# An attention head loop whose rows on ScalarE, VectorE, GpSimdE and the transfer queue are written out, instead of TensorE's alone

## The chip, the cores and the metric

One core of a Trainium2 chip runs the whole program. The metric is the device time of one execution in microseconds, as a median over runs. TensorE (PE) multiplies matrices, ScalarE (ACT) and VectorE (DVE) work on rows of 128 partitions, GpSimdE (POOL) does a few copies and products, and SyncE (SP) issues the transfers.

## The reference

Two residual layers on a sequence of 512 frames of width 1024, all in float32, each made of a token mixer and a gated feed-forward part behind a root-mean-square norm. The first layer mixes by causal means over four windows; the second by attention with 16 heads of width 64, with normed q and k, a learned bias by relative position, and a band of nine chunks of 64 frames:

```python
q = head_rmsnorm(q.reshape(B, S, N_HEADS, HEAD_DIM), q_norm)
k = head_rmsnorm(k.reshape(B, S, N_HEADS, HEAD_DIM), k_norm)
...
s = jnp.einsum('bqhd,bkhd->bhqk', qc, kb).astype(jnp.float32) * scale + bias[None]
s = jnp.where(valid[None, None, None, :], s, -1e30)
p = jax.nn.softmax(s, axis=-1).astype(vb.dtype)
return jnp.einsum('bhqk,bkhd->bqhd', p, vb)
...
return o @ w_o
```

The feed-forward part is `(silu(causal_dwconv3(h W_gate)) * (h W_val)) W_out` with 2816 inner channels. The order of the program is: pool mixer, feed-forward 0, attention, feed-forward 1. The change lies in `attention()` alone.

## The kernel before, in words

Every float32 product is made of three matmuls: each operand is split into a high part `hi` (rounded, by ACT) and a low part `lo` (the rest, by DVE), and `mm3` (L123 to L125) adds hi·hi, hi·lo and lo·hi. So most matmuls need a copy on ACT and then a subtraction on DVE before them.

*The head loop.* Its 64 tiles are (head h, query tile t of 128 frames); step i of the loop is called slot i, with i = 4h + t. In slot i the program issues `scores` of tile i (two matmuls `sc`, L1062 and L1063), `turn` of tile i - 2 (`tp`, transposes of the softmaxed tile, L1078), and, when i - 4 is the last tile of a head, `mix` of this head (`oo`, eight matmuls against the values, L1090). After the scores DVE adds the bias and takes the row's extreme (L1066), ACT takes the exponential with its row sum (L1068), DVE the reciprocal (L1069), ACT scales (L1070). After the transposes ACT copies the high part (`pt..h`, L102) and DVE takes the low part (`pt..l`, L103). After the mix ACT copies one half (`ob`, L1095) and DVE adds it (`o2`, L1096).

*Pairs.* Two heads make a pair. In slots 8m + 2 and 8m + 3 (`CM = (2, 3)`) the next pair's q and k are put channel-major by `channel_major`: four transposes (`zt`, L1032), the high part on ACT (`zh`, L107 for q, L1036 for k), then on DVE the low part of q (`zl`, L108) or the two low parts of k (`kl`, two instructions, L1039), a copy on POOL (L1043) and two transfers (L1046).

*PSUM.* All of `sc`, `tp`, `zt` and `oo` share a ring of four banks (tag S), in the order of their allocation. A tile that comes four allocations later waits until the last reader of the earlier one is done.

*Side work on TensorE.* Between these steps `fill` deals out matmuls of four long generators, by a due count: the q and k projections of pairs 2 to 7 (`project(1)` to `project(3)`, until slots 3.5, 19.5 and 35.5), then the output projection of pairs 0 to 5 (`outputs`, from slot 35.5 to 72): eight outputs `wo` of four pairs, then eight of two pairs. Pairs 6 and 7 come after the loop. A projection leaves four tiles z, copied on ACT (L966) or DVE (L964), squared on ACT (L956), reduced on DVE (L957), and normed by small operations and a product on POOL (L979). An output is added to the residual X on DVE (L1016). Each pair's mixed heads are split into `two..` (L102, L103) before the output projection reads them; two.. 0 and 1 hold the high parts of pairs 0 to 3, two.. 4 and 5 their low parts.

*What sets the order.* Only TensorE runs in the written order in this loop (`tc.manual_schedule(engines={PE})`). The rows of ACT, DVE, POOL and SP are set by a scheduler that places each instruction by readiness and priority as it sees them.

The due counts and the rings are these lines:

```python
FE = (3.5, 19.5, 35.5)
FO = LAG + 6
CM = (2, 3)
```

Of the kernel before, what the change touches and what calls it, by code (L numbers as in the profile page):

```python
# [17 lines left out]
F32 = mybir.dt.float32  # L18
# [54 lines left out]
def trunk(ctx: ExitStack, tc: tile.TileContext, xt, xT, cols, band, edge, poolw, gv, wout, wqk, wv, wo, rel, out):  # L73
# [15 lines left out]
    def psum(tag, name, bufs=2):  # L89
        return ps.tile([P, S], F32, name=name, tag=tag, bufs=bufs)  # L90
# [30 lines left out]
    def mm3(o, sh, sl, mh, ml, first, last, **how):  # L121

        yield nc.tensor.matmul(o, sh, mh, start=first, stop=False, **how)  # L123
        yield nc.tensor.matmul(o, sh, ml, start=False, stop=False, **how)  # L124
        yield nc.tensor.matmul(o, sl, mh, start=False, stop=last, **how)  # L125
# [791 lines left out]
    def attention():  # L917
# [75 lines left out]

            yield from products(ov, wv[half], f"wv{half}", evict=evict)

        def output(ps_, after=None):

            p0, p1 = ps_[0], ps_[-1] + 1
            n = (p1 - p0) * P
            nd = D // n  # L1000
            w = {}

            def load(d):
                eng = nc.gpsimd if p0 < 6 else None
                w[d] = load_split(wo[d:d + nd, :, p0 * P:p1 * P].rearrange("d p m -> p d m"), D, f"wo{d}_{p0}", eng=eng, eng_hi=eng)

            for d in range(KD):
                if d % nd == 0:
                    if d not in w:
                        load(d)  # L1010
                    hi, lo = w[d]
                o = psum("PQ"[d % 2], f"wo{d}_{p0}")
                for p in ps_:
                    s = slice(d % nd * n + (p - p0) * P, d % nd * n + (p - p0 + 1) * P)
                    yield from mm3(o, hi[:, s], lo[:, s], XS[p], XS[KD + p], p == p0, p == p1 - 1)
                nc.vector.tensor_add(X[d], o, X[d])  # L1016
                if after:
                    after(d)
                    if d == 1:
                        load(nd)  # L1020

        def outputs():
            yield from output(range(4))
            yield from output((4, 5))

        def channel_major(p, i):


            zt = psum("S", f"zt{p}_{i}", 4)
            for t in range(TT):  # L1030
                j = 4 * i + 2 * (p % 2)
                nc.tensor.transpose(zt[:, t * P:(t + 1) * P], Z[p // 2, t][:, j:j + 2, :].rearrange("p h d -> p (h d)"), ident)  # L1032
            zh, z2 = (big.tile([P, S], F32R, name=f"z{c}{p}_{i}", tag="zqk", bufs=8) for c in "h2")
            zl = None if i else g_tile(f"zl{p}_{i}")
            if i:
                nc.scalar.activation(zh, zt, AF.Copy, scale=gq[:, i:i + 1])  # L1036
                for e in range(2):
                    hs = slice(e * HD, (e + 1) * HD)
                    nc.vector.scalar_tensor_tensor(KL[p % 2][e][hs], zt[hs], gq[hs, i:i + 1], zh[hs].bitcast(F32), op0=OP.mult, op1=OP.subtract)  # L1039
            else:  # L1040
                split_scaled(zt, gq[:, i:i + 1], zh, zl)

            nc.gpsimd.tensor_copy(z2[HD:], zh[HD:].bitcast(F32))  # L1043
# [5 lines left out]
        def scores(h, t):  # L1049

            p, e = divmod(h, 2)
            q, k, kl = QK[p, 0][e], QK[p, 1][e], KL[p % 2][e]
            if t == 0:

                base = rdram[h, :]
                for r, n in ((0, S - HD), (HD, S)):
                    nc.sync.dma_start(BT[h % 2][r:r + HD, S - n:], bass.AP(tensor=base.tensor, offset=base.offset + HD, ap=[[1, HD], [1, n]]))
            n = (t + 1) * P
            nw = max(n, 256)

            sc = psum("S", f"sc{h}_{t}", 4)
            nc.tensor.matmul(sc[:, :nw], q[:, t * P:n], k[:, :nw], start=True, stop=False)  # L1062
            nc.tensor.matmul(sc[:, :nw], q[:, t * P:n], kl[:, :nw], start=False, stop=True)  # L1063
            SM[h, t] = s_ = big.tile([P, n], F32, name=f"sb{h}_{t}", tag=f"sb{t}")
            mx = tmp.tile([P, 3], F32, name=f"mx{h}_{t}", tag="mx", bufs=4)
            nc.vector.tensor_tensor_reduce(out=s_[:, :n], in0=sc[:, :n], in1=BT[h % 2][:, :n][:, ::-1], scale=1.0,  # L1066
                                           scalar=3e38, op0=OP.add, op1=OP.min, accum_out=mx[:, 0:1])
            nc.scalar.activation(s_[:, :n], s_[:, :n], AF.Exp, scale=-1.0, bias=mx[:, 0:1], accum_out=mx[:, 1:2])  # L1068
            nc.vector.reciprocal(mx[:, 2:3], mx[:, 1:2])  # L1069
            nc.scalar.activation(s_[:, :n], s_[:, :n], AF.Copy, scale=mx[:, 2:3])  # L1070

        def turn(h, t):

            n = (t + 1) * P
            s_ = SM.pop((h, t))
            tp = psum("S", f"tp{h}_{t}", 4)
            for j in range(t + 1):
                nc.tensor.transpose(tp[:, j * P:(j + 1) * P], s_[:, j * P:(j + 1) * P], ident)  # L1078
            split(tp[:, :n].rearrange("p (j q) -> p j q", q=P), *(x[:, t:4 * t + 1:3] for x in PT[h % 2]))

        def mix(h):

            p, e = divmod(h, 2)
            hs = slice(e * HD, (e + 1) * HD)
            oo = psum("S", f"oo{h}", 4)
            if p not in O2:
                O2[p] = big.tile([P, S], F32, name=f"o2_{p}", tag="o2", bufs=4)
            for c in range(2):
                for j in range(TT):
                    nc.tensor.matmul(oo[:, j * P:], V[j, h // 4][:, h % 4].rearrange("p a d -> p (a d)"),  # L1090
                                     PT[e][c][:, 4 * j:3 * j + TT].rearrange("p t q -> p (t q)"),
                                     start=j == 0 and c == 0, stop=j == TT - 1 and c == 1)
            ob = g_tile(f"ob{h}")
            other = slice(HD - e * HD, 2 * HD - e * HD)
            nc.scalar.activation(ob[hs], oo[other], AF.Copy)  # L1095
            nc.vector.tensor_add(O2[p][hs], oo[hs], ob[hs])  # L1096

        Z, QK, SM = {}, {}, {}
        rcol, r2, late = None, small("r2", TT), []
# [2 lines left out]
            late.pop(0)()  # L1102
        run(values(0, "PQ"))
        for i in range(2):
            channel_major(0, i)
        run(values(1, "SS"))


        tiles_ = [(h, t) for h in range(H) for t in range(TT)]
        nb = len(tiles_)  # L1110
        fillers = [(project(1), 96, -3, FE[0]), (project(2), 96, FE[0], FE[1]), (project(3), 96, FE[1], FE[2]), (outputs(), 144, FE[2], nb + FO)]

        with tc.manual_schedule(engines={mybir.EngineType.PE}):
            cur, done, kept = 0, 0, 0

            def fill(upto):

                nonlocal cur, done
                while cur < len(fillers):
                    g, n, a, b = fillers[cur]  # L1120
                    due = n * (upto - a) / (b - a)
                    while done < min(due, n):
                        next(g)
                        done += 1
                    if upto < b:
                        return
                    run(g)
                    cur, done = cur + 1, 0

            fill(0)  # L1130
            for i in range(nb + LAG + LAGM):
                steps = []
                if i < nb:
                    steps.append(lambda: scores(*tiles_[i]))
                if i % 8 in CM and i // 8 + 1 < NPAIR:
                    steps.append(lambda: channel_major(i // 8 + 1, CM.index(i % 8)))
                j = i - LAG
                if 0 <= j < nb:
                    steps.append(lambda: turn(*tiles_[j]))
                j2 = j - LAGM  # L1140
                if 0 <= j2 < nb and j2 % TT == TT - 1:
                    steps.append(lambda: mix(tiles_[j2][0]))
                for x, step in enumerate(steps):
                    step()
                    if late and x < 2:
                        late.pop(0)()
                    fill(i + (x + 1) / len(steps))

                while 8 * kept + 7 <= j2 and (cur == 3 or cur == 2 and done >= 24 * (kept // 2 + 1)):
                    split(O2[kept], XS[kept], XS[KD + kept])  # L1150
                    kept += 1
            fill(nb + FO)
        assert kept == NPAIR
        return lambda after: output((6, 7), after)

    def last_pairs(rest, c, name):

# [89 lines left out]
```

## Time and profile before

| | |
|---|---|
| median of 3 runs | 972.5 us (971.89, 972.5, 973.37) |
| the profiled execution | 972.12 us, of which its span is 970.3 us |
| PE busy | 961.6 us (99%) |
| DVE busy | 809.6 us |
| ACT busy | 576.6 us |
| POOL busy | 102.9 us |
| head loop, first scores to last mix | 452.5 to 606.3 us of the span |
| scores of slots 34, 42, 50 and 56 start | 538.85, 557.03, 573.11, 585.9 us |

Times in the traces are counted from the span's start. PE's busy share is high by construction: matmuls are pipelined and their ends are modelled, so a busy PE may still be waiting; the distance from one start to the next tells more. A group of a timeline (x2, x3) is several instructions of one form in a row.

### The profile page before, as it was taken

Reading aid. Unit: us, or ns where it says so; the run is one execution under the profiler, and the core shown is the slowest. Engines: PE = TensorE matmul, PEld = TensorE weight load, DVE = VectorE, ACT = ScalarE, POOL = GpSimd, SP = SyncE. Lnnn points to the kernel's source line nnn. Section 1 sums busy time; section 2 is a strip of 40 time slices with the busy share of each in tenths; the row PEclk is TensorE's granted clock in tenths of the full one; section 3 lists DMA queues with packets and bytes.
Section 4 is the critical chain, followed back from the end, with each engine's and each line's share of the span. In section 5 each row is a group of like instructions: output and inputs, shape, how many; then the busy total and the mean of one; then the engine's idle time right before and its main releaser. Section 6 shows DMA issues by size and latency. Waiting matters only on the chain.

```text
span 970.3 us, 13704 instructions
## 1 busy us (share of the span) xinstructions
PE 961.6 (99%) x4982; PEld 815.0 (84%) x4982; DVE 809.6 (83%) x1462; ACT 576.6 (59%) x990; POOL 102.9 (11%) x90
## 2 busy tenths in 40 slices
PE   8999999999999999999999999999999999999998
PEld 7788988888888888888888787888988888888886
DVE  8999999999899854442777888999999999989953
ACT  7665564655555544345898988646565565566531
POOL 2300000000000013204534532000000000000000
PEclk9999999999999999999999999999999999999999
DMA  9222332332323224232343341332233233332323
GB/s 342 77 93 71 114 113 75 120 120 92 105 76 120 78 84 147 94 121 91 111 115 107 97 118 55 101 108 80 94 114 104 87 120 108 104 103 77 116 79 109
DMA packets 37427, 102.82 MB, mean 106 GB/s; under 512 B 4432, under 2 KB 7904, under 8 KB 37360
## 3 DMA queue, kind: packets, MB, share of 16 engines
q1 hardware_dynamic: 37296, 101.90, 33.0%
q8 instruction: 39, 0.64, 0.3%
q14 instruction: 28, 0.23, 0.1%
q0 software_dynamic: 32, 0.04, 0.0%
q10 hardware_dynamic: 32, 0.00, 0.0%
HBM read 95.60 MB, written 2.14 MB: 101 GB/s over the span
## 4 chain that ended last, share of the span: by engine, by line
PE 94%; DVE 4%; ACT 2%; issue 0%; DMA 0%; DVEq 0%; ACTq 0%
PE st_m L610 11%; PE out L124 8%; PE out L123 8%; PE out L125 8%; PE st_m L612 6%; PE st_t L610 6%; PE gv L124 4%; PE gv L123 4%; PE gv L125 4%; PE qk L124 3%; PE qk L123 3%; PE qk L125 3%; PE st_t L612 3%; PE st_b L610 3%; PE tp L1078 2%; PE oo L1090 2%
## 5 line engine op out<-in xcount | busy, mean ns | idle before, releaser
L124 PE MATMUL out<-one,ow_h 128*128 128x512 f32 x224 | 87.9, 393 | 0.0
L123 PE MATMUL out<-one,ow_h 128*128 128x512 f32 x224 | 87.8, 392 | 0.0
L125 PE MATMUL out<-one,ow_l 128*128 128x512 f32 x224 | 87.8, 392 | 0.0
L833 DVE TENSOR_TENSOR X<-out,X 128x512 f32<-128x512 f32 (+1 forms) x65 | 44.1, 680 | 49.1 <-PE out L125 48.9
L409 ACT ACTIVATE ow_h<-wo_r 128x640 fp32r<-128x640 f32 (+1 forms) x64 | 50.4, 788 | 56.4 <-PE out L124 46.8
L610 PE MATMUL st_m<-two,g_h 128*128 128x512 f32 x240 | 75.1, 394 | 0.0
L610 PE MATMUL st_m<-h,g_h 128*128 128x512 f32 x240 | 74.0, 389 | 0.0
L410 DVE TENSOR_TENSOR ow_l<-wo_r,ow_h 128x640 fp32r<-128x640 f32 (+1 forms) x64 | 56.5, 883 | 2.5 <-ACT ow_h L409 2.5
L424 DVE SCALAR_TENSOR_TENSOR c<-a,col,c 128x511 f32<-128x511 f32 (+1 forms) x76 | 56.3, 743 | 0.0
L610 PEld LDWEIGHTS st_m<-h,g_h 128*128 128x128 f32 x240 | 45.1, 188 | 10.3
L612 PEld LDWEIGHTS st_m<-two,g_l 128*128 128x128 f32 x240 | 45.0, 188 | 9.5
L610 PEld LDWEIGHTS st_m<-two,g_h 128*128 128x128 f32 x240 | 44.0, 188 | 10.4 <-ACT w L619 0.8
L619 ACT ACTIVATE w<-st_m 128x512 f32<-128x512 f32 x30 | 17.9, 598 | 56.8 <-PE st_m L612 56.8
L125 PE MATMUL qk<-wqk_h,two 128*128 128x512 f32 x128 | 51.4, 402 | 0.0
L123 PE MATMUL qk<-wqk_h,two 128*128 128x512 f32 x128 | 50.8, 409 | 0.0
L124 PE MATMUL qk<-wqk_l,two 128*128 128x512 f32 x128 | 50.8, 397 | 0.0
L612 PE MATMUL st_m<-h,g_l 128*128 128x256 f32 x240 | 48.3, 283 | 0.0
L125 PEld LDWEIGHTS out<-one,ow_l 128*128 128x128 f32 x224 | 42.3, 189 | 6.3
L124 PEld LDWEIGHTS out<-one,ow_h 128*128 128x128 f32 x224 | 42.3, 189 | 6.3 <-DVE one L435 0.3
L612 PE MATMUL st_m<-two,g_l 128*128 128x256 f32 x240 | 47.6, 280 | 0.0
L123 PEld LDWEIGHTS out<-one,ow_h 128*128 128x128 f32 x224 | 42.3, 189 | 6.0
L1066 DVE CUSTOM_DVE_ANT_0 sb<-sc,B 128x128 f32<-128x128 f32 (+1 forms) x64 | 31.1, 486 | 18.9 <-PE sc L1063 18.1
(378 smaller groups left out, 2928.6 us busy)
## 6 DMA issues: line engine op xcount, KB each, us to landing
gv_r<-gv SPq DMA_DIRECT2D x86, 512.0 KB, 3.9
wo_r<-wout SPq DMA_DIRECT2D x32, 384.0 KB, 3.1
wo_r<-wout SPq DMA_DIRECT2D x32, 320.0 KB, 2.9
wqk_r<-wqk SPq DMA_DIRECT2D x16, 512.0 KB, 3.4
wv_r<-wv SPq DMA_DIRECT2D x8, 512.0 KB, 3.3
wo_r<-wo SPq DMA_DIRECT2D x8, 512.0 KB, 3.4
xt<-xt SPq DMA_DIRECT2D x4, 512.0 KB, 5.1
X<-xT SPq DMA_DIRECT2D x8, 256.0 KB, 7.4
```

The lines of the kernel that those rows point to most:

```text
L123: yield nc.tensor.matmul(o, sh, mh, start=first, stop=False, **how)
L124: yield nc.tensor.matmul(o, sh, ml, start=False, stop=False, **how)
L125: yield nc.tensor.matmul(o, sl, mh, start=False, stop=last, **how)
L409: nc.scalar.activation(hi[:, :n], raw[:, :n], AF.Copy)
L410: return hi, lo, lambda: nc.vector.tensor_sub(lo[:, :n], raw[:, :n], hi[:, :n].bitcast(F32))
L424: nc.vector.scalar_tensor_tensor(c[:, j:], a[:, :S - j], cw[2 - j], c[:, j:], op0=OP.mult, op1=OP.add)
L610: nc.tensor.matmul(o, hi[:, c], B[i, name], start=first and i == 0, stop=False, **how)
L612: nc.tensor.matmul(o[:, 0], lo[:, c], B[i, name][:, 0], start=False, stop=i == 3, **how)
L833: nc.vector.tensor_add(X[d][:, fs], o[:, fs], X[d][:, fs])
L1066: nc.vector.tensor_tensor_reduce(out=s_[:, :n], in0=sc[:, :n], in1=BT[h % 2][:, :n][:, ::-1], scale=1.0, scalar=3e38, op0=OP.add, op1=OP.m ...
L1078: nc.tensor.transpose(tp[:, j * P:(j + 1) * P], s_[:, j * P:(j + 1) * P], ident)
L1090: nc.tensor.matmul(oo[:, j * P:], V[j, h // 4][:, h % 4].rearrange("p a d -> p (a d)"), PT[e][c][:, 4 * j:3 * j + TT].rearrange("p t q -> ...
```

## The change

The loop now puts all five rows under manual order: PE, DVE, ACT, POOL and SP issue in the order in which the program writes it. To write that order, the tile's work is turned into a generator with a stop after each step (`tile_of`), `channel_major` likewise (`stages`), and a slot is made of two half slots (`place` 2i and 2i + 1). What isn't a tile's own step (copies and squares of z, reductions, norms, splits of pairs, additions to X, zh, zl, kl, the copy behind a mix) is queued with `later("A", ...)` or `later("D", ...)`, for ACT or DVE, at least a half slot behind the step that it needs, and taken from the queue by `extra`, one or two per half slot. The diff, cut to its core:

```diff
+        def later(engine, fn, n=1):
+            waiting[engine].append((place + n, fn))
+
+        def extra(engine, all_=False):
+
+            n = 0
+            q = waiting[engine]
+            while q and q[0][0] <= place and (n == 0 or all_ or len(q) > 1 and n < 2):
+                q.pop(0)[1]()
+                n += 1
...
+            def scale():
+                next(g)
+                later("D", low)
+
+            def low():
+                next(g)
+                later("D", lambda: run(g), 2)
+
+            later("A", scale)
...
-        with tc.manual_schedule(engines={mybir.EngineType.PE}):
+        order = {mybir.EngineType.PE, mybir.EngineType.DVE, mybir.EngineType.Activation, mybir.EngineType.Pool, mybir.EngineType.SP}
+        with tc.manual_schedule(engines=order):
...
             for i in range(nb + LAG + LAGM):
-                steps = []
...
+                place = 2 * i
+                step(i, "scores")
+                if i % 4 == 2 and i // 4 + 1 < H:
+                    biases(i // 4 + 1)
+                step(i - 1, "recip")
+                step(i - 3, "hi")
+                step(i - 1, "scale")
+                extra("A")
+                extra("D")
+                step(i, "bias")
+                fill(i + 0.45)
                 if i % 8 in CM and i // 8 + 1 < NPAIR:
-                    steps.append(lambda: channel_major(i // 8 + 1, CM.index(i % 8)))
+                    stages(i // 8 + 1, CM.index(i % 8))
+                place = 2 * i + 1
+                step(i, "exp")
+                step(i - LAG, "turn")
+                step(i - 3, "lo")
+                extra("D")
+                extra("A")
+                fill(i + 0.9)
+                j2 = i - LAG - LAGM
                 if 0 <= j2 < nb and j2 % TT == TT - 1:
-                    steps.append(lambda: mix(tiles_[j2][0]))
+                    mix(tiles_[j2][0])
+                fill(i + 1)
```

Further parts of the diff. The first group of outputs takes outputs 0 and 1 together: pairs 0, 1 and 2 for both, then pair 3 for both (`output_heads` with `late = 2`). The loads of the projections' weights are asked for two blocks ahead (`ask`, `chunk`), and their parts (`parts`) are split on ACT and POOL, from block 12 on wholly on POOL, but for the last block, k = 19, which is split on ACT and DVE; so the first half of the weights of the last outputs (pairs 6 and 7, block 18) moves from ACT and DVE to POOL. The loads of the next feed-forward's first weights (gv) are issued behind the loop's own.

Three places show how the rows move; the names carry head and tile (sc9_1 is tile 1 of head 9).

TensorE at the start of the output projection, slots 37 to 39 before: `wo0_0` is output 0 of pairs 0 to 3, `two1_97` the high and `two5_101` the low parts, first of pair 2 and then (from the second L123 row on) of pair 3.

```order
L1063 MATMUL sc9_1_5432<-kl01_3630,z24_0_5078 128x256
L123 MATMUL wo0_0_5379<-two1_97,wo0_0_h_5374 128x512
L124 MATMUL wo0_0_5379<-two5_101,wo0_0_h_5374 128x512
L1078 MATMUL tp8_3_5443<-ident_106,sb8_3_5341 128x128 x4
L125 MATMUL wo0_0_5379<-two1_97,wo0_0_l_5375 128x512
L123 MATMUL wo0_0_5379<-two1_97,wo0_0_h_5374 128x512
L1062 MATMUL sc9_2_5452<-z24_1_5110,z24_0_5078 128x384
L1063 MATMUL sc9_2_5452<-kl01_3630,z24_0_5078 128x384
L124 MATMUL wo0_0_5379<-two5_101,wo0_0_h_5374 128x512
```

After, pair 3 in the same output, slots 40 and 41:

```order
L1046 MATMUL sc10_0_5505<-zh5_1_5356,zh5_0_5322 128x256
L1047 MATMUL sc10_0_5505<-kl10_3631,zh5_0_5322 128x256
L123 MATMUL wo0_0_5367<-two1_97,hw12_h_5267 128x512
L124 MATMUL wo0_0_5367<-two5_101,hw12_h_5267 128x512
L1062 MATMUL tp9_2_5518<-ident_106,sb9_2_5454 128x128 x3
L125 MATMUL wo0_0_5367<-two1_97,hw12_l_5268 128x512
L123 MATMUL wo1_0_5399<-two1_97,hw12_h_5267 128x512
```

The first use of pair 3's low part has moved from just behind the scores of tile 2 of head 9 (slot 38) to just behind those of tile 0 of head 10 (slot 40).

VectorE in slots 42 to 44, before; `sb` is written by the bias step, `zl6` and `kl00`, `kl01` belong to pair 6, `pt0l` is a low part of the softmaxed tile.

```order
L1066 ISA sb10_2_5554,mx10_2_5555<-sc10_2_5551,B0_3637 128x384
L103 TENSOR_TENSOR pt1l_3628<-tp9_3_5534,pt1h_3627 128x4x128
L1069 RECIPROCAL mx10_2_5555<-mx10_2_5555 128x1
L1066 ISA sb10_3_5584,mx10_3_5585<-sc10_3_5581,B0_3637 128x512
L108 SCALAR_TENSOR_TENSOR zl6_0_5568<-zt6_0_5561,gq_109,zh6_0_5566 128x512
L103 TENSOR_TENSOR pt0l_3626<-tp10_0_5576,pt0h_3625 128x128
L1039 SCALAR_TENSOR_TENSOR kl00_3629<-zt6_1_5591,gq_109,zh6_1_5596 64x512
L1039 SCALAR_TENSOR_TENSOR kl01_3630<-zt6_1_5591,gq_109,zh6_1_5596 64x512
L1069 RECIPROCAL mx10_3_5585<-mx10_3_5585 128x1
```

After:

```order
L1051 ISA sb10_2_5559,mx10_2_5560<-sc10_2_5550,B0_3637 128x384
L1068 TENSOR_TENSOR pt1l_3628<-tp9_3_5539,pt1h_3627 128x4x128
L1056 RECIPROCAL mx10_2_5560<-mx10_2_5560 128x1
L1026 SCALAR_TENSOR_TENSOR zl6_0_5571<-zt6_0_5564,gq_109,zh6_0_5569 128x512
L1051 ISA sb10_3_5587,mx10_3_5588<-sc10_3_5579,B0_3637 128x512
L1068 TENSOR_TENSOR pt0l_3626<-tp10_0_5573,pt0h_3625 128x128
L1056 RECIPROCAL mx10_3_5588<-mx10_3_5588 128x1
L1024 SCALAR_TENSOR_TENSOR kl00_3629<-zt6_1_5596,gq_109,zh6_1_5601 64x512
L1024 SCALAR_TENSOR_TENSOR kl01_3630<-zt6_1_5596,gq_109,zh6_1_5601 64x512
```

The low part of q (`zl`) has moved ahead of the bias of slot 43, and the reciprocal of slot 43 ahead of the two low parts of k.

ScalarE in the same slots, before:

```order
L1068 ACTIVATE sb10_2_5554,mx10_2_5555<-sb10_2_5554,mx10_2_5555 128x384
L107 ACTIVATE zh6_0_5566<-zt6_0_5561,gq_109 128x512
L102 ACTIVATE pt0h_3625<-tp10_0_5576 128x128
L1070 ACTIVATE sb10_2_5554<-sb10_2_5554,mx10_2_5555 128x384
L1036 ACTIVATE zh6_1_5596<-zt6_1_5591,gq_109 128x512
L1068 ACTIVATE sb10_3_5584,mx10_3_5585<-sb10_3_5584,mx10_3_5585 128x512
L102 ACTIVATE pt0h_3625<-tp10_1_5605 128x2x128
```

After:

```order
L1054 ACTIVATE sb10_2_5559,mx10_2_5560<-sb10_2_5559,mx10_2_5560 128x384
L1018 ACTIVATE zh6_0_5569<-zt6_0_5564,gq_109 128x512
L1066 ACTIVATE pt0h_3625<-tp10_0_5573 128x128
L1058 ACTIVATE sb10_2_5559<-sb10_2_5559,mx10_2_5560 128x384
L1054 ACTIVATE sb10_3_5587,mx10_3_5588<-sb10_3_5587,mx10_3_5588 128x512
L1018 ACTIVATE zh6_1_5601<-zt6_1_5596,gq_109 128x512
L1066 ACTIVATE pt0h_3625<-tp10_1_5604 128x2x128
```

The exponential of slot 43 and the second high part (`zh6_1`) have changed places.

More of the change, by code (lines that the diff above doesn't have):

```diff
@@ L994, in values, with last_output @@
             yield from products(ov, wv[half], f"wv{half}", evict=evict)
[L996 to L1005, printed above, removed]
-            for d in range(KD):
[L1008 to L1015, printed above, removed]
-                nc.vector.tensor_add(X[d], o, X[d])
[L1017 to L1024, printed above, removed]
+        def last_output(after):
+            for d in range(KD):
+                hi, lo = w[18 + d // 4]
+                o = psum("PQ"[d % 2], f"wo{d}_6")
+                for p in (6, 7):
+                    s = slice((d % 4 * 2 + p - 6) * P, (d % 4 * 2 + p - 5) * P)
+                    yield from mm3(o, hi[:, s], lo[:, s], XS[p], XS[KD + p], p == 6, p == 7)
+                nc.vector.tensor_add(X[d], o, X[d])
+                after(d)
+                if d == 1:
+                    parts(19)
         def channel_major(p, i):
@@ L1113, in attention @@
-        with tc.manual_schedule(engines={mybir.EngineType.PE}):
[L1114 to L1128, printed above, removed]
+        place = 0
@@ new lines, in attention, with step, split_pair, hi @@
+        gens = {}
+        def step(j, name):
+            if 0 <= j < nb:
+                if j not in gens:
+                    assert all((tiles_[j][0] // 2, i) in QK for i in range(2))
+                    gens[j] = tile_of(*tiles_[j])
+                assert next(gens[j]) == name
+        def split_pair(p):
+            def hi():
+                nc.scalar.activation(XS[p], O2[p], AF.Copy)
+                later("D", lo)
+            def lo():
+                nc.vector.tensor_sub(XS[KD + p], O2[p], XS[p].bitcast(F32))
+                kept.add(p)
+            later("A", hi)
@@ L1143, in attention @@
[L1143 to L1154, printed above, removed]
+                place = 2 * i
```

215 lines of the change are left out of this document (187 added, 28 removed).

## The prediction

> **What bounds the kernel now.** I read the page's totals first, then the table of stretches over the head loop, then TensorE's waits there, then the timelines of PE, DVE and ACT around single slots. A slot is one of the 64 steps of the loop (head h, query tile t, number 4h+t).
>
> From the page: the span and the busy time of each engine.
>
> ```profile
> span 970.3 us, 13704 instructions
> PE 961.6 (99%) x4982; PEld 815.0 (84%) x4982; DVE 809.6 (83%) x1462; ACT 576.6 (59%) x990; POOL 102.9 (11%) x90
> ```
>
> PE is busy 99% of the span, so a gain can come only from gaps in PE's row, and a loss only from new ones. PE issues the same matmuls after the change as before, in nearly the same row. The table of stretches (columns: length, then busy time of PE, weight loads, DVE, ACT, POOL, the granted clock, DMA share, GB/s) says where gaps can be:
>
> ```profile
> 540.00:560.00 20.00, 19.08 (x110) 15.36 (x108) 17.25 (x54) 18.05 (x48) 10.12 (x10) 1.00 0.29 77
> 560.00:580.00 20.00, 19.96 (x116) 16.49 (x115) 17.55 (x52) 17.28 (x45) 7.89 (x7) 1.00 0.47 128
> 580.00:605.00 25.00, 24.53 (x137) 20.06 (x135) 19.89 (x61) 21.97 (x56) 7.41 (x4) 1.00 0.22 66
> ```
>
> These are the slots with the output projection as side work. The clock is full. DVE and ACT are 80 to 90% busy, so their orders matter. The waits of PE in the loop that the profile names:
>
> ```profile
> PE wo L124 <- DVE two L103: 0.7, 1, 0.7
> PE oo L1090 <- DVE pt1l L103: 0.5, 1, 0.5
> PE tp L1078 <- ACT sb L1070: 0.5, 2, 0.3
> ```
>
> That is 1.7 us. It is too little, since a matmul's modelled end covers the start of a wait: 512 columns take 0.39 to 0.48 us in a row, yet the next starts earlier. So I count from start to start. PE's timeline, around the waits and in the last outputs of the projection:
>
> ```profile
> 545.19 0.40 PE L123 MATMUL wo<-two,wo_h 128*128 128x512 f32 x1
> 545.70 0.52 PE L1078 MATMUL tp<-ident,sb 128*128 128x128 f32 x3
> ...
> 547.58 0.48 PE L125 MATMUL wo<-two,wo_l 128*128 128x512 f32 x1
> 548.10 0.50 PE L123 MATMUL wo<-two,wo_h 128*128 128x512 f32 x1
> ...
> 548.60 0.34 PE L1063 MATMUL sc<-kl,z 128*128 128x384 f32 x1
> 549.61 0.49 PE L124 MATMUL wo<-two,wo_h 128*128 128x512 f32 x1 [0.66 <-DVE two L103]
> ...
> 559.92 0.47 PE L124 MATMUL wo<-two,wo_h 128*128 128x512 f32 x1
> 560.38 0.41 PE L1078 MATMUL tp<-ident,sb 128*128 128x128 f32 x2
> 560.54 0.47 PE L125 MATMUL wo<-two,wo_l 128*128 128x512 f32 x1
> 561.04 0.76 PE L1090 MATMUL oo<-pt1h,one 128*128 128x512 f32 x3
> ...
> 576.61 0.48 PE L124 MATMUL wo<-two,wo_h 128*128 128x512 f32 x1
> 577.11 0.76 PE L1090 MATMUL oo<-pt1h,one 128*128 128x512 f32 x3
> ...
> 611.64 0.39 PE L123 MATMUL wo<-two,wo_h 128*128 128x512 f32 x1
> ...
> 617.99 0.39 PE L125 MATMUL wo<-two,wo_l 128*128 128x512 f32 x1
> ```
>
> The last two rows are 28 matmuls apart: 0.227 us each, the pace where nothing waits (0.17 for 384 columns). What a start is later than that is wait:
>
> - Start of the output projection: 0.51 - 0.23, 0.52 - 0.23 and 1.01 - 0.17, together 1.4 us. The last is the low part of pair 3, which the first product needs.
> - Slot 42 (the next pair's transposes and heads 10 and 9 meet): 0.23 + 0.27 = 0.50. Slot 50 repeats it (577.11 shows the second half): 0.50. Together 1.00.
> - The end of the loop: the named 0.5 + 0.5. At the start of the projection the view named 0.7 of what starts count as 0.84, so I scale by 1.2: 1.2 us.
>
> In all **3.6 us** of removable wait. PE cannot win more than about this.
>
> **The change part by part.** *What goes.* The first output group now takes two outputs together and brings pair 3's products last, about two slots later (the row of PE in the section on the change): 1.4 goes. At the end of the loop the last head's mix comes later among the products, so the low parts have time: 1.2 goes. The waits of slots 42 and 50 (1.00) go in their old form, as their causes swap: the second transpose then waits for zl, and the mix for the bias of slot 43. Sum: -3.6, if nothing else is late.
>
> *What comes.* The scheduler had chosen by readiness; now ACT and DVE keep the written order. With four banks in the S ring, the transposes of slot 42's tile (tp, two slots later) take the bank of zt, so they wait for the second kl. Rows of before at slot 42, PE, ACT and DVE:
>
> ```profile
> 557.03 0.34 PE L1062 MATMUL sc<-zh,zh 128*128 128x384 f32 x1
> ...
> 563.34 0.49 PE L1078 MATMUL tp<-ident,sb 128*128 128x128 f32 x3
> ```
>
> ```profile
> 558.19 0.62 ACT L1068 ACTIVATE sb<-sb,mx 128x384 f32<-128x384 f32 x1 [0.21 <-DVE mx L1066]
> ...
> 558.81 0.67 ACT L107 ACTIVATE zh<-zt,gq 128x512 fp32r<-128x512 f32 x1
> ...
> 560.84 0.71 ACT L1068 ACTIVATE sb<-sb,mx 128x512 f32<-128x512 f32 x1
> ...
> 561.54 0.37 ACT L102 ACTIVATE pt0h<-tp 128x256 fp32r<-128x256 f32 x1
> ```
>
> ```profile
> 557.59 0.56 DVE L1066 CUSTOM_DVE_ANT_0 sb<-sc,B 128x384 f32<-128x384 f32 x1 [0.15 <-PE sc L1063]
> ...
> 560.14 0.75 DVE L108 SCALAR_TENSOR_TENSOR zl<-zt,gq,zh 128x512 f32<-128x512 f32 x1
> 560.81 0.28 DVE L103 TENSOR_TENSOR pt0l<-tp,pt0h 128x128 fp32r<-128x128 f32 x1
> 561.00 1.50 DVE L1039 SCALAR_TENSOR_TENSOR kl<-zt,gq,zh 64x512 fp32r<-64x512 f32 x2
> 562.54 0.16 DVE L1069 RECIPROCAL mx<-mx 128x1 f32<-128x1 f32 x1
> ```
>
> Before, kl ended 562.50, 5.47 us after the scores, because DVE took the bias of slot 43 ahead of zl, and ACT took the second zh ahead of exp. Now each follows the other in one chain: scores to bias 0.56 (557.03 to 557.59), bias to exp 0.60, exp to zh 0.62 (558.19 to 558.81), zh to zl 0.70 (0.67 and a hand-over of 0.03, an estimate), zl to the bias of slot 43 0.67 (560.14 to 560.81), that bias to its exp 0.73 (0.60 and 0.13 for the 128 columns more, an estimate), exp to second zh 0.70 (560.84 to 561.54), zh to kl 0.70, both kl 1.54 (561.00 to 562.54). Sum 6.82 us. PE wants this tp after 563.34 - 557.03 - 0.50 of wait = 5.81 us. New wait at slot 42: **1.0 us**. At slot 50 the written order also puts an addition to X (taken as 0.6, like the reduction below) between zl and the bias: **1.6**. Half of such a wait falls at the mix, which now waits for the bias, the rest at tp; the sum is the same.
>
> Earlier slots give PE more time. Slot 18 and slot 34 begin here, and the tp of slot 18 here:
>
> ```profile
> 500.06 0.34 PE L1062 MATMUL sc<-zh,zh 128*128 128x384 f32 x1
> ...
> 507.12 0.49 PE L1078 MATMUL tp<-ident,sb 128*128 128x128 f32 x3
> ...
> 538.85 0.34 PE L1062 MATMUL sc<-zh,zh 128*128 128x384 f32 x1
> ```
>
> Slot 18: 7.06 us. Slots 10 and 26 have the same room, against 6.82: no wait. At slots 18 and 34 ACT's order has a copy of z ahead of the second zh, taken as 0.5 us (zh, of the same size, lasts 0.67 and overlaps its neighbours): 7.32, so **0.3** at slot 18. At slot 34 PE wants tp after 545.70 - 538.85 - 0.28 = 6.57: **0.75**.
>
> Slots 35 to 40: DVE also gets the leftover reductions and the norm there. Two neighbours in DVE's timeline give one side operation's step:
>
> ```profile
> 538.55 0.68 DVE L957 TENSOR_REDUCE qk_s<-zs 128x8 f32<-128x512 f32 x1
> 539.14 0.15 DVE L1069 RECIPROCAL mx<-mx 128x1 f32<-128x1 f32 x1
> ```
>
> At 0.59 each, the five of the written order in slots 36 to 39 (a copy, two reduces, o, pair 3's low part) are 3.0 us. The norm's six small ones at up to the 0.15 of a reciprocal are 0.7, and four biases, low parts and reciprocals about 4.0 (by width, between 0.28 and 0.75 a row). That makes 7.7 us. PE's work for a head is 15.8 projection matmuls at 0.227, scores worth 5.5 and a mix worth 5 of them, and ten transposes at about half of one: 7.1 us. So DVE slips by about **0.5**, paid at the scores of slot 40. A lateness from slots 34 and 35 on top may last to slot 42: 0 to 2.4 more.
>
> The end: a low part of gv now stands between the additions and the last weights' low part on DVE.
>
> ```profile
> 611.09 2.35 DVE L103 TENSOR_TENSOR gv_l<-gv_r,gv_h 128x1024 fp32r<-128x1024 f32 x2
> ...
> 616.10 1.22 DVE L103 TENSOR_TENSOR wo_l<-wo_r,wo_h 128x1024 fp32r<-128x1024 f32 x1
> ```
>
> From 611.64 the first output ends about 10 matmuls (2.4 us) in; then an addition 0.6, gv_l 1.17, an addition 0.6, a scaled low part 0.67 (as zl), the weights' 1.22: ready at 618.3, wanted at 617.99, **0.3**. The first half of these weights goes to POOL, hidden: POOL has 7.41 busy of 25 us, and its result is wanted only at 611.64. The SP queue keeps loads in an order that asks two blocks ahead; I price it at nothing, its cover is those two blocks (a late one would cost some 1 to 2 us).
>
> Sum: -3.6 + 1.0 + 1.6 + 0.3 + 0.75 + 0.5 + 0.3 = +0.85 us, and I add 0.4 for part of the carried lateness: +1.2. The profiled execution took 972.12 (span 970.3), near the median 972.5 (971.89 to 973.37): **973.4 us**.
>
> [...]
>
> **The rivals.** *Faster.* The chain is shorter than I sum, or PE itself runs later than I think, so the new waits are about 0.8 us in all: 972.1 - 3.6 + 0.8 = 969.3, at best 968.5. For it: DVE still idles 2.5 to 3 us of each 20 in the table, and queueing side work half a slot late keeps heads of queues ready. Against: the chain holds hardly any side work, and its nine steps come from rows. 0.25.
>
> *Slower.* DVE's and ACT's lateness of slots 34 to 39 isn't absorbed and meets the chain at slot 42: 2.4 us on top of +0.85 gives 975.4; with a second carry into slot 50 about 976.8. It decides where DVE's side work in a stretch exceeds what PE's time leaves, over 7.1 us per head. For it: DVE 17.25 of 20 at 540. Against: before, DVE was idle at times there, and the gaps can take it. 0.32.
>
> *No change in kind.* PE's instructions are the same, so the orders elsewhere don't matter beyond small shifts: 972.5. This lies in the middle case, with the forecast: 0.43.
>
> **How the numbers follow.** A difference under 0.2% (1.9 us: 970.6 to 974.4) can't be told from none. Forecast and no change together have 0.43, mostly within that; the first rival 0.25, faster; the second 0.32, slower. The range goes from 969.0, just under the first rival's time, to 976.5, just under the second's far end, which leaves about 0.2 out.
>
> **What would show it.** In the changed profile: no wait of wo for two at the start of the projection; none of oo for pt1l at the end; new waits of tp for kl (and of oo for the bias) at slots 42 and 50 of about 1.0 and 1.6, and 0.75 at slot 34; DVE with zl ahead of the bias of slot 43, and kl ending 6.8 us after the scores of slot 42. I am wrong if kl ends under 6 us there, if the waits stay where they were, or if the largest loss lies in POOL's or SP's rows.

## The result, and the profile after

The changed kernel takes 980.13 us (median of 4, 980.06 to 980.4) against 972.19 us for the kernel before beside it: a ratio of 1.008, with a 95% interval of 1.0062 to 1.0097. It is 8 us slower. The forecast was 973.4 us, with a range up to 976.5. The page's totals after the change:

```profile
span 978.3 us, 13709 instructions
PE 963.7 (98%) x4982; PEld 815.6 (83%) x4982; DVE 811.7 (83%) x1461; ACT 576.5 (59%) x989; POOL 105.7 (11%) x92
```

But for the half of the last weights that POOL now splits (two instructions more), no engine has more work. The span grew by 8.0 us (978.3 against 970.3) while PE's busy time grew by 2.1, so the loss is waiting. The table of stretches shows where; columns as in the prediction. First two rows of before, then four after the change:

```profile
500.00:520.00 20.00, 20.00 (x112) 16.91 (x112) 17.69 (x52) 19.71 (x48) 9.78 (x8) 1.00 0.32 100
520.00:540.00 20.00, 20.00 (x112) 16.85 (x112) 13.99 (x42) 17.08 (x41) 7.79 (x6) 1.00 0.41 131
```

```profile
500.00:520.00 20.00, 19.14 (x106) 15.92 (x105) 15.75 (x45) 17.08 (x44) 8.42 (x8) 1.00 0.33 81
520.00:540.00 20.00, 17.89 (x97) 14.39 (x96) 15.02 (x39) 16.32 (x39) 8.90 (x7) 1.00 0.35 96
540.00:560.00 20.00, 18.61 (x105) 15.09 (x104) 16.68 (x51) 17.20 (x45) 7.45 (x7) 1.00 0.35 99
560.00:580.00 20.00, 18.18 (x104) 14.52 (x103) 16.06 (x48) 17.12 (x44) 10.17 (x9) 1.00 0.35 89
```

PE now idles from 500 to 540 us too, while the q and k projections run, where before it was busy throughout, and the clock stays at 1.00. The waits of PE in the loop and behind it, by what ended them:

```profile
PE tp L1062 <- DVE kl L1024: 3.5, 5, 0.8
PE sc L1046 <- DVE mx L1051: 2.6, 3, 1.3
PE tp L1062 <- DVE zl L1026: 0.7, 2, 0.5
PE sc L1046 <- DMA zh<-zh: 0.3, 1, 0.3
PE oo L1080 <- DVE mx L1051: 0.3, 1, 0.3
PE oo L1080 <- DVE pt1l L1068: 0.3, 1, 0.3
PE wo L125 <- DVE hw_l L103: 0.2, 1, 0.2
PE tp L1062 <- DVE pt1l L1068: 0.2, 1, 0.2
```

All three waits named before have left their places or shrunk: wo for pair 3's low part is gone, tp for ACT's sb too, and oo for pt1l has gone from 0.5 to 0.3. But the list now sums to 8.1 us instead of 1.7, and all of it but 0.3 us (a transfer) is for VectorE. The starts of the scores, from the two timelines, say when the loss comes:

| scores of slot | 16 | 24 | 28 | 36 | 42 | 48 | 56 | 63 | next feed-forward |
|---|---|---|---|---|---|---|---|---|---|
| before, us | 496.05 | 515.46 | 525.57 | 544.71 | 557.03 | 570.01 | 585.86 | 598.32 | 622.52 |
| after, us | 496.26 | 516.81 | 529.44 | 549.09 | 561.82 | 577.11 | 594.40 | 606.29 | 630.49 |
| later by | 0.21 | 1.35 | 3.87 | 4.38 | 4.79 | 7.10 | 8.54 | 7.97 | 7.97 |

The largest steps are slots 24 to 28 (2.5 us), 42 to 48 (2.3), 48 to 56 (1.4) and 16 to 24 (1.1). Slots 16, 24, 40 and 48 each begin a block of eight, in whose third and fourth slots the next pair is transposed.

Slot 42 again, DVE first; the rows are the sum behind a mix, an addition to X, the bias of slot 41, a second addition, the bias of slot 42, zl, the bias of slot 43 and both kl. Then PE's scores of slot 42, those of slot 43, and the transposes of slot 42's tile:

```profile
561.02 0.68 DVE L1091 TENSOR_TENSOR o<-oo,ob 64x512 f32<-64x512 f32 x1 [0.80 <-ACT ob L1087]
...
561.70 0.66 DVE L1240 TENSOR_TENSOR X<-wo,X 128x512 f32<-128x512 f32 x1
562.29 0.41 DVE L1051 CUSTOM_DVE_ANT_0 sb<-sc,B 128x256 f32<-128x256 f32 x1
...
563.45 0.67 DVE L1240 TENSOR_TENSOR X<-wo,X 128x512 f32<-128x512 f32 x1
564.03 0.55 DVE L1051 CUSTOM_DVE_ANT_0 sb<-sc,B 128x384 f32<-128x384 f32 x1
...
565.95 0.75 DVE L1026 SCALAR_TENSOR_TENSOR zl<-zt,gq,zh 128x512 f32<-128x512 f32 x1 [0.41 <-ACT zh L1018]
566.61 0.68 DVE L1051 CUSTOM_DVE_ANT_0 sb<-sc,B 128x512 f32<-128x512 f32 x1
...
568.76 1.51 DVE L1024 SCALAR_TENSOR_TENSOR kl<-zt,gq,zh 64x512 fp32r<-64x512 f32 x2 [0.41 <-ACT zh L1018]
```

```profile
561.82 0.38 PE L1046 MATMUL sc<-zh,zh 128*128 128x384 f32 x1
...
564.65 0.50 PE L1046 MATMUL sc<-zh,zh 128*128 128x512 f32 x1 [0.56 <-DVE mx L1051]
...
570.42 0.30 PE L1062 MATMUL tp<-ident,sb 128*128 128x128 f32 x1 [0.77 <-DVE kl L1024]
```

From the bias of slot 42 (564.03) to the end of kl (570.27) it is 6.24 us. The prediction's chain without its first step is 6.26. The chain is as long as it was summed. But it begins 2.21 us after the scores instead of 0.56, and so kl ends 8.45 us after them, not 6.8. Of these 1.65 us the two additions to X that stand ahead of the biases in DVE's written order are 1.2 (0.59 and 0.58, from start to next start). The other 0.5 is lateness that DVE brought along; the sum o in the first row had waited 0.80 us for ACT. And PE waited one time more than forecast: the scores of slot 43 now also wait for the bias of slot 42 (the line sc for mx).

Slots 26 and 27 hold the largest step. DVE's rows there (the low part of a finished pair, that of a softmaxed tile, that of another finished pair, the bias of slot 26), POOL's row beside them, two rows of ACT, and PE's:

```profile
520.20 0.67 DVE L1296 TENSOR_TENSOR two<-o,two 128x512 fp32r<-128x512 f32 x1
...
522.10 0.56 DVE L1068 TENSOR_TENSOR pt1l<-tp,pt1h 128x384 fp32r<-128x384 f32 x1 [0.89 <-ACT pt1h L1066]
522.58 1.98 DVE L1296 TENSOR_TENSOR two<-o,two 128x512 fp32r<-128x512 f32 x1
...
524.56 0.53 DVE L1051 CUSTOM_DVE_ANT_0 sb<-sc,B 128x384 f32<-128x384 f32 x1
```

```profile
521.63 2.38 POOL L103 TENSOR_TENSOR hw_l<-hw_r,hw_h 128x1024 fp32r<-128x1024 f32 x1 [1.36 <-ACT hw_h L102]
```

```profile
520.51 1.05 ACT L102 ACTIVATE hw_h<-hw_r 128x1024 fp32r<-128x1024 f32 x1
521.58 0.49 ACT L1066 ACTIVATE pt1h<-tp 128x384 fp32r<-128x384 f32 x1
```

```profile
523.41 0.40 PE L125 MATMUL qk<-hw_h,two 128*128 128x512 f32 x1
525.15 0.50 PE L1046 MATMUL sc<-zh,zh 128*128 128x512 f32 x1 [1.34 <-DVE mx L1051]
```

The low part of a pair lasts 1.98 us instead of the 0.67 us of its neighbour at 520.20. It ends 0.55 us after POOL's instruction (521.63 + 2.38 = 524.01), a little less than the time that it takes alone. This text calls that a hold. The bias behind it is late by the difference, 1.3 us, and PE stands for 1.34 us. The hold isn't all: the bias of slot 26 starts 3.61 us after its scores (520.95), and DVE had also stood 0.89 us for pt1h, which ACT took behind a copy of weights of 1.05 us. Neither was a step of the prediction.

### The profile page after: what moved, and what is told of

It is laid out like the page before. It is cut to its first block, busy times and chain, and to the rows that moved or that the text cites. A ratio compares the mean times of both kernels' runs of the same rounds, so it can differ in the third digit from the quotient of the medians.

```text
span 978.3 us, 13709 instructions
## 1 busy us (share of the span) xinstructions
PE 963.7 (98%) x4982; PEld 815.6 (83%) x4982; DVE 811.7 (83%) x1461; ACT 576.5 (59%) x989; POOL 105.7 (11%) x92
## 4 chain that ended last, share of the span: by engine, by line
PE 86%; DVE 6%; ACT 4%; issue 2%; DMA 1%; SPq 0%; DVEq 0%; ACTq 0%
PE st_m L610 11%; PE out L124 8%; PE out L123 8%; PE out L125 8%; PE st_m L612 6%; PE st_t L610 6%; PE gv L124 4%; PE gv L125 4%; PE gv L123 4%; PE st_t L612 3%; PE st_b L610 3%; PE qk L123 2%; PE qk L125 2%; PE qk L124 2%; PE v L124 1%
## 5 line engine op out<-in xcount | busy, mean ns | idle before, releaser
L123 PE MATMUL out<-one,ow_h 128*128 128x512 f32 x224 | 87.9, 392 | 0.0
L103 POOL TENSOR_TENSOR hw_l<-hw_r,hw_h 128x1024 fp32r<-128x1024 f32 x19 | 45.9, 2417 | 51.9 <-ACT hw_h L102 51.3
L1054 ACT ACTIVATE sb<-sb,mx 128x128 f32<-128x128 f32 (+1 forms) x64 | 35.9, 560 | 23.9 <-DVE mx L1051 23.5
L123 PEld LDWEIGHTS out<-one,ow_h 128*128 128x128 f32 x224 | 42.4, 189 | 6.1
L421 ACT ACTIVATE c<-a,col 128x512 f32<-128x512 f32 x38 | 30.7, 814 | 25.1 <-DVE a L768 23.5
```

The source lines that it names most:

```text
L103: return (eng or nc.vector).tensor_sub(lo, raw, hi.bitcast(F32))
L1054: nc.scalar.activation(s_, s_, AF.Exp, scale=-1.0, bias=mx[:, 0:1], accum_out=mx[:, 1:2])
```

## The experiments

Three causes were to be told apart: the longer chain (the prediction's), side work ahead of the bias, and DVE operations held beside POOL. The rival to all of them was that TensorE's own new row or the loads cost the time. Times are medians, ratios are against the kernel before on the same chip. The intervals reach 0.9 to 1.7 us to each side, so single differences of under 1 us between two variants are not told apart.

**Whose rows?** The first kernel keeps all of the change but the manual order of the four other engines:

```diff
-        order = {mybir.EngineType.PE, mybir.EngineType.DVE, mybir.EngineType.Activation, mybir.EngineType.Pool, mybir.EngineType.SP}
+        order = {mybir.EngineType.PE}
```

> The changed kernel with the written order kept on TensorE alone; the scheduler places ScalarE, VectorE, GpSimdE and the transfers again. Theory (the written rows of VectorE and ScalarE hold what TensorE needs): the new waits of tp for kl (3.5 us) and of sc for the bias (2.6 us) go, 970 to 973 us. Rival (the loss lies in TensorE's own new row or in the weights' new loads and splits): it stays at 978 to 981 us.

Measured: 972.95 us, ratio 1.0005 (0.9996 to 1.0015). So the loss lies in the four written rows, up to 0.7 us that can't be told from nothing. TensorE's new row, the regrouped outputs and the new loads cost nothing that can be measured, and win nothing either. Two more kernels free one row each:

> The changed kernel with VectorE's row placed by the scheduler again; TensorE, ScalarE, GpSimdE and SyncE keep the written order. Theory (VectorE's written row holds most of it, since all the waits but a few are named after VectorE): 973 to 976 us. Rival (ScalarE's written row, with the exponential ahead of the second high part, suffices): 977 to 980 us.

> The changed kernel with ScalarE's row placed by the scheduler again; TensorE, VectorE, GpSimdE and SyncE keep the written order. Theory (both rows hold each other: with VectorE's row free, 977.7 us): 974 to 978 us, with the waits of sc for the bias left and less of tp for kl. Rival (ScalarE's row costs nothing): 979.5 to 981 us.

Measured: 977.72 us (1.0057, 1.0042 to 1.0072) with DVE's row free, 979.54 us (1.0071, 1.0056 to 1.0087) with ACT's row free. DVE's row alone gives back 2.4 us, less than its theory asked, and falls in the rival's range; ACT's alone gives 0.6, again in the rival's. Freed together with POOL and SP they give 7.2. With DVE free, ACT's fixed row is waited for (tp for sb on ACT, 3.2 us), so the two rows bind each other and neither alone holds the loss. POOL's and SP's rows were not freed by themselves; but a kernel below that keeps them written comes within 1.3 us of before, so they can't hold much more than that.

**The chain.** At slots 8m+2 and 8m+3 the second zh goes ahead of the exponential, zl behind the bias, and kl ahead of the reciprocal, as the scheduler had them:

```diff
-        gens = {}
+        gens, urgent = {}, []
...
             def scale():
                 next(g)
-                later("D", low)
+                if i:
+                    urgent.append(low)
+                else:
+                    later("D", low, 2)
...
-            later("A", scale)
+            if i:
+                scale()
+            else:
+                later("A", scale)
...
+                while urgent:
+                    urgent.pop()()
                 step(i - 1, "recip")
```

> The changed kernel with the order of before at slots 8m+2 and 8m+3 alone: the second high part ahead of the exponential, the low part of q behind the bias, the low parts of k ahead of the reciprocal. Theory of the prediction (the chain of 6.8 us is the loss): kl ends about 1.4 us earlier at each of six pairs, most of the 3.5 us of tp waiting for kl goes, 975 to 977 us. Rival (VectorE is late already when the chain starts, by side work): under 1.5 us is won, 978.5 to 980 us.

Measured: 980.76 us (1.0084, 1.0069 to 1.0099). No wait of tp for kl is left, as the theory said, and the transposes of slot 18 come 7.03 us after its scores instead of 8.00. Yet the median did not move; it lies above the rival's range too. The profile is of the shortest of the four executions (979.08 us; the others took 980.64 to 981.28), so what the others lost besides is not shown. Its first waits, and its longest held operation with POOL's row beside it:

```profile
PE sc L1046 <- DVE mx L1051: 3.3, 4, 2.0
PE qk L123 <- DVE z L1157: 1.2, 1, 1.2
```

```profile
522.32 2.61 DVE L1296 TENSOR_TENSOR two<-o,two 128x512 fp32r<-128x512 f32 x1
```

```profile
522.01 2.37 POOL L103 TENSOR_TENSOR hw_l<-hw_r,hw_h 128x1024 fp32r<-128x1024 f32 x1
```

The pair's low part now starts 0.31 us into POOL's instruction instead of 0.95, and lasts 2.61 us. This hold, a late copy of z at slots 4 to 6, behind the loop's first transposed pair (1.2 us), and late biases took most of what the chain had won.

**The holds.** Two kernels. The first issues the splits of weight blocks 10 and 11 five matmuls later:

```diff
-                        if n == 8:
+                        if n == (13 if k in (9, 10) else 8):
                             parts(k + 1)
```

> The changed kernel with the splits of weight blocks 10 and 11 issued five matmuls later, so that GpSimdE's low part no longer runs beside VectorE's low part of a pair (1.98 us and 1.87 us instead of 0.69). Theory (VectorE is held while GpSimdE works): both return to 0.7 us, and slots 26 to 28, which lost 3.0 us against before, give 1 to 2.5 us back: 977.5 to 979 us. Rival (the rows' order alone): no change, 980 us.

Measured: 978.58 us (1.0067, 1.0052 to 1.0082), 1.5 us less than the change and where its theory put it. (By the starts of the scores, slots 26 to 28 had lost 2.4 us, not 3.0.) The same operation, now ahead of POOL's row:

```profile
521.27 0.68 DVE L1296 TENSOR_TENSOR two<-o,two 128x512 fp32r<-128x512 f32 x1
```

```profile
522.57 2.40 POOL L103 TENSOR_TENSOR hw_l<-hw_r,hw_h 128x1024 fp32r<-128x1024 f32 x1 [2.66 <-ACT hw_h L102]
```

Apart in time it takes 0.68. Slot 28 is 2.01 us later than before instead of 3.87. But the edit moves ACT's copy of these weights too, and DVE no longer stands for pt1h there: the bias of slot 26 starts 1.4 us after its scores, not 3.61. The gain is not the hold's alone by this run. The second kernel leaves the weights where they were and computes the low part of each pair on POOL, so that DVE has no such operation:

```diff
-                nc.vector.tensor_sub(XS[KD + p], O2[p], XS[p].bitcast(F32))
+                nc.gpsimd.tensor_sub(XS[KD + p], O2[p], XS[p].bitcast(F32))
```

> The changed kernel with the low part of each finished pair computed on GpSimdE instead of VectorE, the one VectorE operation of the loop's side work whose two inputs both lie in SBUF beside GpSimdE's low parts. [...] Rival (only a delay of GpSimdE's row in exchange): 979.5 to 981 us, with zt or sc waiting for GpSimdE.

Measured: 979.25 us (1.0073, 1.0058 to 1.0088), 0.25 us under the rival's range, and zt and sc don't wait for POOL. The holds are gone with the operation. With ACT's copy still in its place, the bias of slot 26 starts 2.0 us after its scores, 1.6 us less, and slot 28 is 1.95 us later than before: here it is the hold that went, with the 0.6 us of the operation itself. Slot 34 is 1.9 us earlier than with the change, but the last weights' low part came later: wo waited 1.2 us for it instead of 0.2.

**Together.** The short chain with the pairs' low part on POOL, then also side work behind the bias:

```diff
                 extra("A")
+                step(i, "bias")
                 extra("D")
-                step(i, "bias")
```

> The changed kernel with the order of before at slots 8m+2 and 8m+3 and the pairs' low part on GpSimdE. Theory (the chain and the holds are two causes, and the holds ate what the short chain won): 973.5 to 976 us. Rival (neither matters beyond shifting waits): 978.5 to 981 us.

> As the kernel with the order of before at slots 8m+2 and 8m+3 and the pairs' low part on GpSimdE, and VectorE's other side work behind the bias of its slot. Theory (side work ahead of the bias is the third cause: sc waited 3.3 us for the bias with the short chain): 970 to 973 us. Rival (VectorE has too little room in slots 35 to 44, in any order): 974 to 976 us.

> The changed kernel with one swap: VectorE's queued side work is issued behind the bias of the slot instead of ahead of it (this moves the low part of q behind the bias of slot 8m+3 as well). Theory (side work ahead of the bias makes the chain at slots 8m+2 late: the bias starts 1.13 us after the scores at slot 18 and 2.21 us at slot 42, against 0.56): sc no longer waits for the bias, tp for kl less, 974 to 977 us. [...]

Measured: 977.12 us (1.005, 1.0033 to 1.0067), short of its theory by 1.1 us, and 975.55 us (1.0035, 1.0022 to 1.0048), which is the rival's range. Alone the short chain had won nothing and the pairs' low part on POOL 0.9 us, together they win 3.0: the holds had eaten what the chain won. Side work behind the bias adds 1.6. It is less than hoped: the late copy of z at slots 4 to 6 and the last weights' late low part (1.2 us each) are still there, and zt at slot 42 now waits for POOL. The last of the three expectations is for the swap alone on the changed kernel: 980.81 us (1.0086, 1.0069 to 1.0102), nothing won. The bias of slot 18 does start 0.56 us after its scores again, and that of slot 42 1.06. But the execution that was profiled is the longest of the four (983.45 us; the others took 980.26 to 981.3). In it the scores waited 2.3 us for a transfer of zh, where with the change they waited 0.3. What the other three executions lost is not shown. The next kernel keeps each correction only where it had not cost: the chain for pairs 2 to 7, POOL for the low part of pairs 0, 1, 2, 4 and 5, the swap from slot 8 on.

> The changed kernel with the three corrections together, each kept from the place where it cost something: the order of before at slots 8m+2 and 8m+3 for pairs 2 to 7 only, the pairs' low part on GpSimdE for pairs 0, 1, 2, 4 and 5 only, side work behind the bias from slot 8 on. Theory (the corrections add up; the 1.5 us of slots 3 to 6, the last weights' 1.0 us and part of zt's wait for GpSimdE go against the last kernel of this kind): 971.5 to 973.5 us. Rival (TensorE only meets the next wait in the row): 974.5 to 976 us.

Measured: 973.46 us (1.0011, 1.0002 to 1.002). This is the theory's range, at its end. Three corrections to the order and to one operation's engine undo 6.7 of the 8 us. Slots 8 to 42 are within 0.5 us of before (slot 42 at 556.99 against 557.03). How the 6.7 us divide among the three stays open, as they help or spoil each other. What is left begins in slot 42:

```profile
PE zt L1014 <- POOL z L1195: 1.2, 2, 0.7
```

Two more kernels went after that wait. One leaves side work ahead of the bias in slots 35 to 41, the other takes the last projection's reductions and norm ahead of other side work.

> As the kernel with the three corrections together, but in slots 35 to 41 side work stays ahead of the bias, so that the norm of the last projection comes earlier. Theory (zt at slot 42 waits 1.2 us for GpSimdE's product because the norm is late): zt's wait goes, 0.5 to 1.2 us less than without this. Rival (the bias of slots 38 to 41 is late instead): the same or 0.5 us more.

> As the kernel with the three corrections together, and the reductions and the norm of the last projection taken from the queues ahead of other side work. Theory (the last 1.2 us over before is zt of slots 42 and 43 waiting for GpSimdE's product behind a late norm): that wait shrinks by about the time of one slot, 1.2 us or more, 971.5 to 972.5 us. Rival (the two slots are bound by the bias, the queue only changes which wait ends last): 973 to 974 us.

Measured: 973.86 us (1.0016, 1.0007 to 1.0025) and 973.82 us (1.0021, 1.0012 to 1.003), both in their rivals' ranges. In the first of them zt still waits 0.7 us for POOL, and the scores now wait 1.1 us for late biases, as its rival has it. In the second zt waits no more, but POOL's products of z now run beside the low part of pair 3, which is still on DVE:

```profile
554.53 1.55 DVE L1301 TENSOR_TENSOR two<-o,two 128x512 fp32r<-128x512 f32 x1
```

```profile
554.49 2.49 POOL L1200 TENSOR_TENSOR z<-z,qk_y 128x512 f32<-128x512 f32 x2 [5.57 <-DVE qk_y L1198]
```

and wo waits 1.5 us for that low part. So the hold came back in a new place. Whether any written row of slots 36 to 44 does better than the scheduler's stays open.

**The promised gain.** The regrouping of the first outputs, put into the kernel before alone:

```diff
+                oo2 = [psum("PQ"[d], f"wo{d}_{p0}") for d in range(2)]
+                for ps in (ps_[:-1], ps_[-1:]):
+                    for p, d in [(p, d) for p in ps for d in range(2)] if len(ps) > 1 else [(ps[0], 0), (ps[0], 1)]:
...
+                        yield from mm3(oo2[d], hi[:, s], lo[:, s], XS[p], XS[KD + p], p == p0, p == p1 - 1)
```

> The kernel before with one part of the change: the first output group takes outputs 0 and 1 together and pair 3 last; all else is placed as before. The prediction's first term: the wait of 0.84 us for pair 3's low part goes and with it up to 1.4 us at the start of the projection, 970.9 to 971.8 us. Rival (another wait takes its place): within 0.4 us of before.

Measured: 972.27 us, ratio 0.9997 (0.9988 to 1.0006): the rival. Its waits:

```profile
PE tp L1090 <- ACT sb L1082: 1.5, 4, 0.8
PE oo L1102 <- DVE pt1l L103: 0.5, 1, 0.5
```

The 0.7 us of wo for pair 3's low part is gone, and tp's wait for ACT grew from 0.5 to 1.5 us. The scores of slot 63 come only 0.4 us earlier, counted from slot 0, of the 1.4 us in the sum.

## Why the prediction was wrong

The direction of the sum was right and its chain is there, but it put the loss at 1.2 us where 8.0 came. Two steps failed: the chain was let start on time in every block, and 3.6 us were counted as gain. By its steps:

- *What goes, 3.6 us.* Wrong in size. Of the 1.4 us at the start of the projection, 0.4 came where only the outputs were regrouped, and nothing that the total shows: another wait, of tp for ACT, ended in its place. Of the 1.2 at the end of the loop about 0.6 came (slots 56 to 63 in the table). The 1.0 of slots 42 and 50 was not tried alone. The kernel with TensorE's new row and the scheduler's other rows is no faster than before. To count a wait as a gain, one has to show what is late next; the text says "if nothing else is late" and then does not ask.
- *The chain, 6.82 us.* Right, and not by luck. Where the bias did start 0.55 to 0.61 us after the scores, at slots 10, 34 and 50, kl ended 6.81, 7.33 and 7.40 us after them, where the sums give 6.82, 7.32 and 7.42. At slot 42 it is 6.24 us from the bias on, against 6.26. The order of before at these slots removed the wait of tp for kl.
- *"Slots 10 and 26 have the same room, against 6.82: no wait", 0.3 at slot 18, 1.0 at slot 42.* This is the step that failed, but for slot 10, where the transposes came 7.02 us after the scores, as forecast. It let the chain start 0.56 us after the scores, as in before. In the written order side operations stand ahead of the bias, and the bias began 1.13 us after the scores at slot 18 (a reduction at 500.86, the bias at 501.47, the scores at 500.34), 3.61 at slot 26 and 2.21 at slot 42. The measured steps in the table are 1.1 us (slots 16 to 24), 2.5 (24 to 28) and 2.3 (42 to 48), about 6 of the 8 us.
- *The hold.* Not in the sum, and most of the step at slot 26: with the pairs' low part on POOL slots 24 to 28 lose 1.0 us instead of 2.5. A row of before shows such a hold: the low part of a pair took 1.55 us there, beside POOL's products, while the mean over the seven of this form was 0.81. The first of the four products took 1.04 us, to 514.89, and the low part ended 0.55 us after it.

```profile
513.89 1.55 DVE L103 TENSOR_TENSOR two<-o,two 128x512 fp32r<-128x512 f32 x1
```

```profile
513.85 4.50 POOL L979 TENSOR_TENSOR z<-z,qk_y 128x512 f32<-128x512 f32 x4 [5.56 <-DVE qk_y L977]
```

- *0.75 at slot 34, 0.5 for slots 35 to 40, 1.6 at slot 50.* About right as costs. The scores of slot 40 waited 0.65 us for a bias, where 0.5 was forecast. Slots 28 to 42 lost 0.9 us; with the costs of 1.25 that leaves a gain of about 0.3 of the 1.4 forecast. Slots 48 to 56 lost 1.4, where 1.6 less 0.5 was forecast.
- *The end.* Right: wo waited for the last weights' low part (0.2, forecast 0.3), oo for pt1l less.
- *The rivals.* The second (lateness met by the chain) was what happened, but it was priced at 2.4 us more and placed at slots 34 to 44 alone. The lateness began in slot 18. The third, that orders elsewhere don't matter, is refuted: TensorE's row is the same with the other rows free and with them written, and 7.2 us lie between.

## What to carry to other kernels

When a scheduler's order is replaced by a written one, sum each stretch with the side work that the new order puts ahead of the first link, not the bare chain. Look for the rows that last far above their group's mean before pricing a new neighbour of theirs: here a mean of 0.81 us over a form hid a hold of 1.55. And a wait that goes is a gain only up to the next wait behind it.

## What the runs showed of the hardware

A pair's low part on VectorE, with both inputs in SBUF, was held while GpSimdE ran an instruction. The four rows of it in the kernels before and after that lasted 0.8 us or more, and one each with the short chain and with DVE's row free, all began beside an instruction of GpSimdE and finished 0.54 to 0.56 us after it (an end is the start and the length added up):

| kernel | low part starts | lasts, us | POOL's instruction | POOL ends | low part ends later by |
|---|---|---|---|---|---|
| before | 513.89 | 1.55 | z, the first of four | 514.89 | 0.55 |
| after | 522.58 | 1.98 | hw_l | 524.01 | 0.55 |
| after | 533.80 | 1.87 | hw_l | 535.12 | 0.55 |
| after | 590.18 | 0.96 | hw_h | 590.60 | 0.54 |
| short chain | 522.32 | 2.61 | hw_l | 524.38 | 0.55 |
| DVE's row free | 585.51 | 2.87 | hw_l | 587.82 | 0.56 |

The last of them:

```profile
585.51 2.87 DVE L1296 TENSOR_TENSOR two<-o,two 128x512 fp32r<-128x512 f32 x1
```

```profile
585.44 2.38 POOL L103 TENSOR_TENSOR hw_l<-hw_r,hw_h 128x1024 fp32r<-128x1024 f32 x1
```

585.44 + 2.38 = 587.82, and DVE ended at 588.38. The other twelve low parts of the kernels before and after took 0.67 to 0.69 us. One of these began 0.07 us before the end of a product of POOL (520.20 in the changed kernel) and ended 0.60 us after it; another began 0.03 us ahead of a subtraction of POOL that lasted 2.93 us (582.04 in the kernel before) and took 0.68. So in these traces the low part never ended before an instruction of GpSimdE beside which it began.

Two operations of DVE with at most one input in SBUF kept their time beside POOL's subtractions and products, in the changed kernel's loop. Six additions to X, with the other input in PSUM, that began beside one took 0.67 us on average, the nine that began beside nothing of POOL 0.68. Of the reductions, with one input in SBUF, five took 0.68 us beside one, seven 0.68 apart. Why the low part is held and these are not, no run shows.
